# Transposes of activations moved from TensorE to VectorE, in 32 x 32 squares, in a hybrid transformer block

## The chip, the cores and the metric

The kernel runs on one core of a Trainium2 chip. The metric is the device time of one execution in microseconds (us), the median of several runs. The profile is of one execution; its times are in us from the span's start.

## What is computed

One block of a transformer on 256 tokens of width 2048, all in float32. `h = rmsnorm(x)` is multiplied by a wide matrix; a first branch (four heads, a gated linear attention in chunks of 128 tokens) and a second branch (eight heads of differential attention) come out of it, are gated and added; an output projection goes onto the residual stream, and a feed-forward part with a convolution along the tokens follows.

```python
proj = h @ w_in
a_qk, a_v, a_o, a_if, b_q, b_k, b_v, g_a, g_b = split(proj)
h_m = rmsnorm(mlstm_chunkwise(q_m, k_m, v_m, i_pre, f_pre), mlstm_norm_g)
y_a = sigmoid(a_o) * h_m
q_d, k_d = rmsnorm(b_q, q_norm_g), rmsnorm(b_k, k_norm_g)      # per head, 128 features
y_b = diff_attention(q_d, k_d, v_d, lam, lam_init, subln_g)
x = x + (sigmoid(g_a) * y_a + sigmoid(g_b) * y_b) @ w_out
h = rmsnorm(x, norm2_g)
u_g, u_v = split(causal_dwconv(h @ w_up))
x = x + (silu(u_g) * u_v) @ w_down
```

## The kernel before

Every float32 product is made of three products of float32r numbers: an operand is split into a high part (rounded to float32r) and a low part (what is left), and high x high, high x low and low x high are added up in PSUM. The weights are split as they are streamed: `load_chunk` (L80) loads a raw chunk of 1 MB (512 rows by 512 columns, three buffers), and for each of its two halves ScalarE casts the high part `whi` (L90) and VectorE subtracts it from the raw half, which gives the low part `wlo` (L91). There are four buffers of half chunks for each part.

TensorE's queue is in the order in which the program is written (`manual_schedule`); those of the other engines are put in order by a scheduler, with the preparation of weights 100 instructions ahead of other work (`AHEAD`). `t_block` (L101) makes a block of 256 tokens by 512 columns: four chunks, each of two halves of 12 products (L112 to L114). `f_group` (L118) and `wide_group` (L625) do the same with features on the partitions. After each half `slots.tick()` counts one tick and runs the side work that was put down for it with `slots.after(n, ...)`: small products, transposes and what follows them stand between the halves of the main stream.

A mixer (L527, four of them, each for one head of the first branch and two of the second one) has seven blocks: the first branch's values, the second branch's queries, keys and values, and three gates. Where an activation with tokens on the partitions is needed with features there, TensorE transposes it 128 x 128 at a time against an identity, into a PSUM bank `side`:

- `qk_norm` (L447): queries and keys are normed on VectorE to `qn` [128, 2, 4, 128] (L458). Four ticks later `turn` (L461) transposes them, eight times (L465), and ScalarE writes them, scaled by the gain, to `qT` or `kT` (L466).
- the end of `mixer`: the mixed states `hm` of 512 features. Four ticks later `turn` (L565) transposes them, eight times (L570); ScalarE casts the high part `yh` (L574), VectorE subtracts for the low part `yl` (L575). The output projection (L592 on) reads those of mixer j in its chunk j; the last mixer's are made in the projection's first block.
- the residual stream after each of the projection's four blocks: `x2` is added up on VectorE (L601), three ticks later `turn` (L607) transposes 512 features, eight times (L613), and ScalarE and VectorE write both parts, scaled by the norm's gain, for the feed-forward part (L143, L144). Its first group reads the parts of block n in its chunk n.

The load of `x` into `x2` (L598) is issued from ScalarE's queue. The attention weights are transposed on TensorE too (L501); so they are in the changed kernel.

Of the kernel before, what the change touches and what calls it, by code (L numbers as in the profile page):

```python
# [11 lines left out]
F32 = mybir.dt.float32  # L12
F32R = mybir.dt.float32r
AF = mybir.ActivationFunctionType
ALU = mybir.AluOpType
# [10 lines left out]
BH, BD = 8, 128  # L26
# column offsets in w_in
O_AV = 2 * AH * AQK
# [8 lines left out]
BIG = 1e30  # L37
# how far the preparation of weights goes ahead of other work, in instructions
AHEAD = 100


class Slots:
    """Side work placed between the half chunks of the main stream of products."""

# [18 lines left out]
def block_kernel(ctx: ExitStack, tc, x, xT, w_in, ifb, qkw, mg, qg, kg, dl, sg, w_out,  # L63
# [14 lines left out]

# [1 line left out]
    def load_chunk(dmas, ahead=AHEAD):  # L80
# [20 lines left out]
    def t_block(w, col, ah, al):  # L101
        """[tokens, 512] = act.T @ w[:, col:col+512], act as [K, tokens] in parts."""
        ps = [acc(), acc()]
        for c in range(4):
            parts = col_chunk(w, c, col)
            for i in range(2):
                for k in (2 * i, 2 * i + 1):
                    whi, wlo = parts[k]
                    first, last = c == 0 and k == 0, c == 3 and k == 3
                    for t in range(2):  # L110
                        tok = slice(t * P, (t + 1) * P)
                        nc.tensor.matmul(ps[t], ah[c][:, k, tok], whi, start=first, stop=False)  # L112
                        nc.tensor.matmul(ps[t], ah[c][:, k, tok], wlo, start=False, stop=False)  # L113
                        nc.tensor.matmul(ps[t], al[c][:, k, tok], whi, start=False, stop=last)  # L114
                slots.tick()
        return ps

    def f_group(load, ah, al, ps=None, chunks=range(4)):  # L118
        """four tiles [128 features, tokens], two to a bank."""
        ps = ps or [acc(), acc()]  # L120
# [15 lines left out]

# [1 line left out]
    def xtiles(c):  # L138
# [6 lines left out]

# [1 line left out]
    warm = const.tile([P, 1], F32, name="warm")  # L147
# [37 lines left out]

# [1 line left out]
    ident = const.tile([P, P], F32, name="ident")  # L187
# [20 lines left out]
    def rstd(out_, ss, n, count):  # L208
        """(ss / count + EPS) ** -0.5, [P, n]"""
        nc.vector.tensor_scalar(out_, ss, 1.0 / count, EPS, ALU.mult, ALU.add)  # L210
        nc.gpsimd.tensor_tensor(out_, out_, mhalf[:, :n], ALU.pow)

    def row_norm(ssq, name):
        """sums of squares [P, 2, 4] -> rs [P, 2] and its rows on all partitions [P, S]"""
        rs = const.tile([P, 2], F32, name=name)
# [44 lines left out]

    # -lambda
    dlb = start.tile([P, 4, BD], F32, name="dlb")
# [16 lines left out]

    # the masks, and the distances of the keys  # L280
    dist = const.tile([P, S], F32, name="dist")
# [4 lines left out]

# [1 line left out]
    tus = [const.tile([P, 2, 3 + S], F32, name=f"tu{i}") for i in range(3)]  # L288
# [8 lines left out]
    def conv(pool, src, rsb, w, ft, taps):  # L297
        """causal convolution along the tokens of two feature tiles [P, 2, S], scaled by rsb"""
        tu = next_tu()
# [14 lines left out]
    def heads(g, ps):  # L314
        for b in range(2):
# [3 lines left out]
            nc.scalar.activation(o, cv, AF.Silu)  # L319
            qk[2 * g + b] = o          # feature tiles 4g+2b, 4g+2b+1: one head  # L320

    def qk_group(g):
        heads(g, f_group(lambda c: col_chunk(w_in, c, g * 512), hh, hl))

# [1 line left out]
    gate = {}  # L326

    def gates():
        # columns 0..3: i, 32..35: f, as they are; 64..67, 96..99: what their float32r parts leave
        ws = []  # L330
# [8 lines left out]
        def rows():  # L339
# [8 lines left out]
            for n, r in enumerate((li, f)):  # L348
# [3 lines left out]
                nc.vector.tensor_scalar_add(r, r, ib[:, n:n + 1])  # L352
            # log sigmoid: min(f, 0) - log(1 + exp(-|f|))
            nc.scalar.activation(e, f, AF.Abs)
            nc.scalar.activation(e, e, AF.Exp, scale=-1.0)
            nc.scalar.activation(e, e, AF.Ln, bias=1.0)
            nc.vector.scalar_tensor_tensor(lf, f, 0.0, e, ALU.min, ALU.subtract)
            # b: sums of lf in each chunk; a = li - b; mx: running maximum of a, with the carried one
            rows3 = pa.tile([AH, 2 * S + S + P], F32, tag="yb", name="rows3")
# [5 lines left out]
            nc.vector.tensor_tensor(a[:, :S], li, b, ALU.subtract)  # L365
            # the keys of the first chunk as the second one sees them
            nc.vector.tensor_scalar_add(a[:, S:], a[:, :P], b[:, P - 1:P])
# [24 lines left out]

# [1 line left out]
    def mlstm(j, v, hm):  # L394
        """hm [P, 2, 512]: normed states of head j"""
        gb = pa.tile([P, AV], F32, tag="gb", name="gb", bufs=1)
# [3 lines left out]
        kw = dict(skip_group_check=True)  # L400
        # blocks (keys, queries): (0, 0), (1, 1), (0, 1)
        for n, mx in enumerate(gate["mx"]):
# [42 lines left out]

# [1 line left out]
    def qk_norm(ps, gain, dst, wait):  # L447
        """tokens on partitions -> normed, [128, 4, tokens]"""
        st = pa.tile([P, 2, 4], F32, tag="st", name="st", bufs=2)
# [10 lines left out]

        def turn():  # L461
            for t in range(2):
                pt = side()
                for g in range(4):
                    nc.tensor.transpose(pt[:, g * P:(g + 1) * P], qn[:, t, g], ident)  # L465
                nc.scalar.activation(dst[:, :, t * P:(t + 1) * P],  # L466
                                     pt.rearrange("p (g s) -> p g s", s=P), AF.Copy, scale=gain[:, 0:1])
        slots.after(wait, turn)

# [1 line left out]
    scale = BD ** -0.5  # L471
# [51 lines left out]

# [1 line left out]
    yh, yl = [], []  # L525

    def mixer(j):  # L527
# [9 lines left out]
        kT = pa.tile([P, 4, S], F32, tag="kT", name="kT")  # L537
        qk_norm(t_block(w_in, O_BQ + j * 512, hh, hl), qgc, qT, 4)
        qk_norm(t_block(w_in, O_BK + j * 512, hh, hl), kgc, kT, 4)
        ps = t_block(w_in, O_BV + j * 512, hh, hl)  # L540
# [23 lines left out]

        def turn():  # L565
            for n in range(2):
                pt = side()
                for m in range(2):
                    for t in range(2):
                        nc.tensor.transpose(pt[:, m * S + t * P:m * S + (t + 1) * P],  # L570
                                            hm[:, t, (2 * n + m) * P:(2 * n + m + 1) * P], ident)
                o = slice(2 * n, 2 * n + 2)
                pv = pt.rearrange("p (m s) -> p m s", s=S)
                nc.scalar.copy(hi[:, o], pv)  # L574
                nc.vector.tensor_tensor(lo[:, o], pv, hi[:, o].bitcast(F32), ALU.subtract)  # L575
        slots.after(4, turn)

# [9 lines left out]

# [1 line left out]
    p2 = ExitStack()  # L589
    ss2 = const.tile([P, 2, 4], F32, name="ss2")  # L590
    z = []
    for n in range(4):  # L592
# [13 lines left out]

        def turn(n=n, hi=hi, lo=lo):  # L607
            for b in range(2):
                pt = side()
                for m in range(2):  # L610
                    k = 4 * n + 2 * b + m
                    for t in range(2):
                        nc.tensor.transpose(pt[:, m * S + t * P:m * S + (t + 1) * P],  # L613
                                            x2[:, t, k * P:(k + 1) * P], ident)
                for m in range(2):
                    k = 4 * n + 2 * b + m
                    split_scaled(hi[:, 2 * b + m], lo[:, 2 * b + m], pt[:, m * S:(m + 1) * S],
                                 g2c[:, k:k + 1])
        slots.after(3, turn)
    p3.close()  # L620
    rs2, rsb2, spread2 = row_norm(ss2, "rs2")
    slots.after(7, spread2)

# [1 line left out]
    def wide_group(w, col, bank):  # L625
        """four tiles [128 features, tokens], one to a bank, from both parts of z side by side:
        the first half of a bank holds hi * hi + lo * hi, the second one hi * lo"""
        ps = [bank() for _ in range(4)]
# [14 lines left out]
    def ffn_conv(ps, ft):  # L643
        """-> two tiles [P, 2, S]"""
        res = []
# [23 lines left out]
    ps = [[acc() if n < 2 else side() for t in range(2)] for n in range(4)]  # L669
    # two k tiles at once where banks come free, and where they are left, one after the other  # L670
    for ks in [(0, 1)] + [(k,) for k in range(2, NFT - 2)] + [(NFT - 2, NFT - 1)]:
# [63 lines left out]
```

## Time and profile before

| | |
|---|---|
| median of 3 runs | 1604.93 us (1604.55 to 1605.22) |
| span of the profiled execution | 1603.3 us; the page gives no other time of it |
| TensorE (PE) busy | 1592.8 us, 99% |
| VectorE (DVE) busy | 1005.6 us, 63% |
| ScalarE (ACT) busy | 832.1 us, 52% |
| GpSimd (POOL) busy | 35.0 us |
| HBM read | 297.44 MB, 187 GB/s over the span |

Busy time of an engine is the union of its instructions. TensorE's products overlap (a product of 512 columns is shown with 0.39 us, while the next one starts 0.23 us after it), so what a product costs is read from start to start. PEld is TensorE's load of the stationary operand, which runs beside the products. An idle time in brackets names the instruction whose end released it.

### The profile page before, as it was taken

Reading aid. Unit: us, or ns where it says so; the run is one execution under the profiler, and the core shown is the slowest. Engines: PE = TensorE matmul, PEld = TensorE weight load, DVE = VectorE, ACT = ScalarE, POOL = GpSimd, SP = SyncE. Lnnn points to the kernel's source line nnn. Section 1 sums busy time; section 2 is a strip of 40 time slices with the busy share of each in tenths; the row PEclk is TensorE's granted clock in tenths of the full one; section 3 lists DMA queues with packets and bytes.
Section 4 is the critical chain, followed back from the end, with each engine's and each line's share of the span. In section 5 each row is a group of like instructions: output and inputs, shape, how many; then the busy total and the mean of one; then the engine's idle time right before and its main releaser. Section 6 shows DMA issues by size and latency. Waiting matters only on the chain.

```text
span 1603.3 us, 20531 instructions
## 1 busy us (share of the span) xinstructions
PE 1592.8 (99%) x8149; PEld 1353.8 (84%) x8149; DVE 1005.6 (63%) x1372; ACT 832.1 (52%) x1135; POOL 35.0 (2%) x54
## 2 busy tenths in 40 slices
PE   8999999999999999999999999999999999999998
PEld 8988888888988888888888888888888888888887
DVE  6865655565655655566555776677767776655554
ACT  6754545454554555455444655555555555444442
POOL 0000000000000000100000000000000000000000
PEclk9999999999999999999999999999999999999999
DMA  9655455545555455554655555555555555555553
GB/s 306 210 192 190 162 195 175 184 166 188 174 181 190 164 187 177 182 184 166 240 176 181 185 186 188 188 189 190 187 184 184 184 184 186 199 193 186 204 187 132
DMA packets 138553, 300.88 MB, mean 188 GB/s; under 512 B 9816, under 2 KB 12120, under 8 KB 132312
## 3 DMA queue, kind: packets, MB, share of 16 engines
q1 hardware_dynamic: 137720, 296.41, 54.7%
q10 hardware_dynamic: 416, 2.11, 0.4%
q0 software_dynamic: 320, 1.05, 0.3%
q8 instruction: 64, 1.05, 0.3%
q14 instruction: 33, 0.27, 0.0%
HBM read 297.44 MB, written 2.10 MB: 187 GB/s over the span
## 4 chain that ended last, share of the span: by engine, by line
PE 98%; DMA 1%; SPq 0%; DVE 0%; ACT 0%; issue 0%
PE acc L112 15%; PE acc L114 15%; PE acc L113 15%; PE side L636 10%; PE acc L636 10%; PE side L638 5%; PE acc L638 5%; PE acc L687 2%; PE acc L688 2%; PE side L688 2%; PE side L687 2%; PE acc L689 2%; PE side L689 2%; PE acc L133 2%; PE acc L131 2%; PE acc L132 2%
## 5 line engine op out<-in xcount | busy, mean ns | idle before, releaser
L91 DVE TENSOR_TENSOR wlo<-raw,whi 128x1024 fp32r<-128x1024 f32 x548 | 670.0, 1224 | 483.3 <-ACT whi L90 481.0
L90 ACT CAST whi<-raw 128x1024 fp32r<-128x1024 f32 x548 | 575.4, 1051 | 634.3 <-PE acc L114 289.0
L112 PE MATMUL acc<-whi,x 128*128 128x512 f32 x896 | 352.8, 394 | 0.0
L114 PE MATMUL acc<-whi,x 128*128 128x512 f32 x896 | 349.4, 390 | 0.0
L113 PE MATMUL acc<-wlo,x 128*128 128x512 f32 x896 | 349.1, 390 | 0.0
L636 PE MATMUL side<-x,whi 128*128 128x512 f32 x704 | 249.2, 399 | 0.0
L636 PE MATMUL acc<-x,whi 128*128 128x512 f32 x704 | 249.2, 399 | 0.0
L114 PEld LDWEIGHTS acc<-whi,x 128*128 128x128 f32 x896 | 168.2, 188 | 35.5
L638 PE MATMUL side<-x,wlo 128*128 128x256 f32 x704 | 197.7, 281 | 0.0
L638 PE MATMUL acc<-x,wlo 128*128 128x256 f32 x704 | 197.5, 281 | 0.0
L112 PEld LDWEIGHTS acc<-whi,x 128*128 128x128 f32 x896 | 168.3, 188 | 34.1
L113 PEld LDWEIGHTS acc<-wlo,x 128*128 128x128 f32 x896 | 168.4, 188 | 33.5
L636 PEld LDWEIGHTS side<-x,whi 128*128 128x128 f32 x704 | 132.3, 188 | 33.0
L636 PEld LDWEIGHTS acc<-x,whi 128*128 128x128 f32 x704 | 132.3, 188 | 32.8
L638 PEld LDWEIGHTS side<-x,wlo 128*128 128x128 f32 x704 | 133.0, 189 | 0.0
L638 PEld LDWEIGHTS acc<-x,wlo 128*128 128x128 f32 x704 | 132.9, 189 | 0.0
L308 DVE SCALAR_TENSOR_TENSOR cv<-tu,fwc,cv 128x256 f32<-128x256 f32 x176 | 73.4, 479 | 0.0
L687 PE MATMUL acc<-whi,ah 128*128 128x512 f32 x176 | 68.5, 389 | 0.0
L689 PE MATMUL acc<-whi,al 128*128 128x512 f32 x176 | 68.5, 389 | 0.0
L688 PE MATMUL acc<-wlo,ah 128*128 128x512 f32 x176 | 68.5, 389 | 0.0
L687 PE MATMUL side<-whi,ah 128*128 128x512 f32 x176 | 68.5, 389 | 0.0
L688 PE MATMUL side<-wlo,ah 128*128 128x512 f32 x176 | 68.5, 389 | 0.0
(209 smaller groups left out, 1646.4 us busy)
## 6 DMA issues: line engine op xcount, KB each, us to landing
raw<-w_in SPq DMA_DIRECT2D x126, 1024.0 KB, 4.9
raw<-w_up SPq DMA_DIRECT2D x88, 1024.0 KB, 5.0
raw<-w_down SPq DMA_DIRECT2D x44, 1024.0 KB, 4.8
raw<-w_out SPq DMA_DIRECT2D x16, 1024.0 KB, 5.0
wr<-w_in SPq DMA_DIRECT2D x8, 256.0 KB, 4.2
xs<-x SPq DMA_DIRECT2D x2, 1024.0 KB, 9.6
x<-x ACTq DMA_DIRECT2D x1, 2048.0 KB, 8.3
out<-x SPq DMA_DIRECT2D x8, 256.0 KB, 2.4
```

The costliest lines, as they stand in the source:

```text
L90: nc.scalar.copy(hi, r)
L91: nc.vector.tensor_tensor(lo, r, hi.bitcast(F32), ALU.subtract)
L112: nc.tensor.matmul(ps[t], ah[c][:, k, tok], whi, start=first, stop=False)
L113: nc.tensor.matmul(ps[t], ah[c][:, k, tok], wlo, start=False, stop=False)
L114: nc.tensor.matmul(ps[t], al[c][:, k, tok], whi, start=False, stop=last)
L131: nc.tensor.matmul(o, whi, ah[c][:, k, :], start=st, stop=False, **kw)
L308: nc.vector.scalar_tensor_tensor(cv[:, f], tu[:, f, 3 - d:3 - d + S], wf[:, j:j + 1], cv[:, f], ALU.mult, ALU.add)
L636: nc.tensor.matmul(ps[f], whi, z[c][:, k].rearrange("p t s -> p (t s)"), start=first, stop=last, skip_group_check=True)
L638: nc.tensor.matmul(ps[f][:, :S], wlo, z[c][:, k, 0], start=False, stop=last, skip_group_check=True)
L687: nc.tensor.matmul(ps[n][t], h_, whi, start=k == 0, stop=False)
L688: nc.tensor.matmul(ps[n][t], h_, wlo, start=False, stop=False)
L689: nc.tensor.matmul(ps[n][t], l_, whi, start=False, stop=k == NFT - 1)
```

## The change

A helper `block_turn` transposes 256 tokens by 512 features on VectorE: a transpose of VectorE turns squares of 32 x 32 within 32 partitions, so 16 instructions, one for each pair of a group of 32 partitions of the source and one of the destination, each of eight squares, put the squares where they belong. Queries and keys, mixed states and residual use it right where they are made, not in a slot some ticks later; ScalarE scales queries and keys in place (one instruction of 1024 elements a partition instead of two of 512 from PSUM), and the parts of the mixed states and of the residual are made from the transposed tile in SBUF. The tile of the mixed states, `yt`, takes the buffer of `kT`; `zt` is new, with two buffers. Comments are left out of the file as well, so its line numbers are other ones.

```diff
+    def block_turn(dst, src):
+        v = dst.rearrange("p m (t s) -> p t m s", t=2)
+        for a in range(4):
+            for b in range(4):
+                nc.vector.transpose(v[32 * b:32 * b + 32, :, :, 32 * a:32 * a + 32],
+                                    src[32 * a:32 * a + 32, :, :, 32 * b:32 * b + 32])
...
-    def qk_norm(ps, gain, dst, wait):
+    def qk_norm(ps, gain, dst):
...
-        def turn():
-            for t in range(2):
-                pt = side()
-                for g in range(4):
-                    nc.tensor.transpose(pt[:, g * P:(g + 1) * P], qn[:, t, g], ident)
-                nc.scalar.activation(dst[:, :, t * P:(t + 1) * P],
-                                     pt.rearrange("p (g s) -> p g s", s=P), AF.Copy, scale=gain[:, 0:1])
-        slots.after(wait, turn)
+        block_turn(dst, qn)
+        nc.scalar.activation(dst, dst, AF.Copy, scale=gain[:, 0:1])
...
-        def turn():
-            for n in range(2):
-                pt = side()
-                for m in range(2):
-                    for t in range(2):
-                        nc.tensor.transpose(pt[:, m * S + t * P:m * S + (t + 1) * P],
-                                            hm[:, t, (2 * n + m) * P:(2 * n + m + 1) * P], ident)
...
-                nc.scalar.copy(hi[:, o], pv)
-                nc.vector.tensor_tensor(lo[:, o], pv, hi[:, o].bitcast(F32), ALU.subtract)
-        slots.after(4, turn)
+        yt = pa.tile([P, 4, S], F32, tag="kT", name="yt")
+        block_turn(yt, hm.rearrange("p t (m f) -> p t m f", f=P))
+        nc.scalar.copy(hi, yt)
+        nc.vector.tensor_tensor(lo, yt, hi.bitcast(F32), ALU.subtract)
...
-        def turn(n=n, hi=hi, lo=lo):
-            for b in range(2):
-                pt = side()
...
-                        nc.tensor.transpose(pt[:, m * S + t * P:m * S + (t + 1) * P],
-                                            x2[:, t, k * P:(k + 1) * P], ident)
...
-        slots.after(3, turn)
+        zt = pb.tile([P, 4, S], F32, tag="zt", name="zt", bufs=2)
+        block_turn(zt, x2[:, :, cs].rearrange("p t (m f) -> p t m f", f=P))
+        for m in range(4):
+            split_scaled(hi[:, m], lo[:, m], zt[:, m], g2c[:, 4 * n + m:4 * n + m + 1])
```

How the instructions stand on the engines is shown at three places. The first is VectorE after the block of queries in the first mixer; before, low parts alone stand behind the second `qn`:

```order
L458 TENSOR_TENSOR qn<-acc,st 128x512
L91 TENSOR_TENSOR wlo<-raw,whi 128x1024
L458 TENSOR_TENSOR qn<-acc,st 128x512
L91 TENSOR_TENSOR wlo<-raw,whi 128x1024 x6
L453 TENSOR_REDUCE st<-sq 128x4
```

and with the change (L398 is the transpose in `block_turn`, L466 the norming):

```order
L466 TENSOR_TENSOR qn<-acc,st 128x512
L398 STREAM_TRANSPOSE qT<-qn 32x2x4x32 x2
L91 TENSOR_TENSOR wlo<-raw,whi 128x1024
L398 STREAM_TRANSPOSE qT<-qn 32x2x4x32 x5
L91 TENSOR_TENSOR wlo<-raw,whi 128x1024
L398 STREAM_TRANSPOSE qT<-qn 32x2x4x32 x5
L91 TENSOR_TENSOR wlo<-raw,whi 128x1024
L398 STREAM_TRANSPOSE qT<-qn 32x2x4x32 x4
L91 TENSOR_TENSOR wlo<-raw,whi 128x1024 x3
L461 TENSOR_REDUCE st<-sq 128x4
```

Sixteen transposes stand among the same six low parts, three of which come between them.

The second place is ScalarE at the same point, with the change. L460 is the square of the norm, L470 the scaling by the gain:

```order
L460 ACTIVATE sq<-acc,rs_577 128x512
L90 CAST whi<-raw 128x1024 x5
L470 ACTIVATE qT<-qT,qgc 128x1024
L90 CAST whi<-raw 128x1024 x2
L460 ACTIVATE sq<-acc,rs_577 128x512
```

Before, two scalings (L466) stood behind four casts and waited for TensorE; now one stands behind five casts and waits for VectorE.

The third place is VectorE from the end of the last mixer through the output projection's first block, with the change (L561 adds the branches, L570 is the low part `yl`, L595 adds the residual `x_6619`, which is `x2`):

```order
L561 TENSOR_TENSOR hm<-hm,yb 128x512
L91 TENSOR_TENSOR wlo<-raw,whi 128x1024
L398 STREAM_TRANSPOSE yt<-hm 32x2x4x32 x5
L91 TENSOR_TENSOR wlo<-raw,whi 128x1024
L398 STREAM_TRANSPOSE yt<-hm 32x2x4x32 x5
L91 TENSOR_TENSOR wlo<-raw,whi 128x1024
L398 STREAM_TRANSPOSE yt<-hm 32x2x4x32 x5
L91 TENSOR_TENSOR wlo<-raw,whi 128x1024
L398 STREAM_TRANSPOSE yt<-hm 32x2x4x32
L91 TENSOR_TENSOR wlo<-raw,whi 128x1024
L570 TENSOR_TENSOR yl_6456<-yt,yh_6455 128x1024
L91 TENSOR_TENSOR wlo<-raw,whi 128x1024 x4
```

Before, four low parts stood between the last addition and the two instructions for `yl`. On ScalarE the cast of `yh` now stands behind five casts of weights, and the load of `x` behind one more cast and with a wait for VectorE.

## Rows read from the trace of the kernel before

**Rows 1.** The page: busy time by engine, granted clock in slices, the chain's shares.
```profile
span 1603.3 us, 20531 instructions
...
PE 1592.8 (99%) x8149; PEld 1353.8 (84%) x8149; DVE 1005.6 (63%) x1372; ACT 832.1 (52%) x1135; POOL 35.0 (2%) x54
...
PEclk9999999999999999999999999999999999999999
...
PE 98%; DMA 1%; SPq 0%; DVE 0%; ACT 0%; issue 0%
```
**Rows 2.** The table of waits: us in total, times, longest.
```profile
DVE wlo L91 <- ACT whi L90: 481.0, 388, 3.2
ACT whi L90 <- PE acc L114: 289.0, 200, 2.4
```
**Rows 3.** Groups by line on PE: count | busy us, mean ns | idle before.
```profile
L465 PE MATMUL side<-ident,qn 128*128 128x128 f32 x64 | 8.3, 272 | 0.0
...
L613 PE MATMUL side<-ident,x 128*128 128x128 f32 x32 | 4.1, 272 | 0.0
L570 PE MATMUL side<-ident,hm 128*128 128x128 f32 x32 | 4.1, 272 | 0.0
```
**Rows 4.** Instructions in order of time, first mixer: start, us, engine, line.
```profile
118.06 0.39 PE L113 MATMUL acc<-wlo,x 128*128 128x512 f32 x1
118.28 0.39 PE L114 MATMUL acc<-whi,x 128*128 128x512 f32 x1
...
119.62 0.40 PE L113 MATMUL acc<-wlo,x 128*128 128x512 f32 x1
```
**Rows 5.** The same in the output projection's first block.
```profile
778.29 0.39 PE L114 MATMUL acc<-whi,yl 128*128 128x512 f32 x1
...
779.63 0.40 PE L113 MATMUL acc<-wlo,yh 128*128 128x512 f32 x1
```
**Rows 6.** Groups by line on DVE.
```profile
L91 DVE TENSOR_TENSOR wlo<-raw,whi 128x1024 fp32r<-128x1024 f32 x548 | 670.0, 1224 | 483.3 <-ACT whi L90 481.0
...
L651 DVE TENSOR_TENSOR u<-acc,u 128x256 f32<-128x256 f32 x44 | 17.0, 423 | 0.4 <-ACT u L650 0.4
...
L144 DVE SCALAR_TENSOR_TENSOR x<-side,g2c,x 128x256 fp32r<-128x256 f32 x16 | 7.0, 478 | 0.6 <-ACT x L143 0.6
...
L601 DVE TENSOR_TENSOR x<-acc,x 128x512 f32<-128x512 f32 x8 | 5.2, 682 | 0.0
```
**Rows 7.** DVE in order of time, feed-forward part.
```profile
906.23 1.12 DVE L651 TENSOR_TENSOR u<-side,u 128x256 f32<-128x256 f32 x3
```
**Rows 8.** DVE and ACT in order of time, queries of the first mixer.
```profile
114.76 0.68 DVE L458 TENSOR_TENSOR qn<-acc,st 128x512 f32<-128x512 f32 x1
...
118.71 1.05 ACT L90 CAST whi<-raw 128x1024 fp32r<-128x1024 f32 x1 [1.67 <-PE acc L114]
...
119.79 1.23 DVE L91 TENSOR_TENSOR wlo<-raw,whi 128x1024 fp32r<-128x1024 f32 x1 [1.49 <-ACT whi L90]
```
**Rows 9.** DVE and ACT in order of time, last mixer's end; the load's landing.
```profile
771.41 1.22 DVE L91 TENSOR_TENSOR wlo<-raw,whi 128x1024 fp32r<-128x1024 f32 x1
...
778.72 1.05 ACT L90 CAST whi<-raw 128x1024 fp32r<-128x1024 f32 x1 [1.75 <-PE acc L114]
779.60 0.39 ACTq L598 DMA_DIRECT2D x<-x  x1
...
DMA to landing us min/median/max: 8.3/8.3/8.3
```
**Rows 10.** PE and ACT in order of time, first feed-forward group.
```profile
860.43 0.39 PE L636 MATMUL acc<-x,whi 128*128 128x512 f32 x1
...
868.83 1.04 PE L613 MATMUL side<-ident,x 128*128 128x128 f32 x8
...
869.86 0.83 ACT L143 ACTIVATE x<-side,g2c 128x256 fp32r<-128x256 f32 x2
```
**Rows 11.** DMA issues: count, KB each, median us to landing.
```profile
raw<-w_in SPq DMA_DIRECT2D x126, 1024.0 KB, 4.9
```

More of the change, by code (lines that the diff above doesn't have):

```diff
@@ L537, in mixer @@
         kT = pa.tile([P, 4, S], F32, tag="kT", name="kT")
-        qk_norm(t_block(w_in, O_BQ + j * 512, hh, hl), qgc, qT, 4)
-        qk_norm(t_block(w_in, O_BK + j * 512, hh, hl), kgc, kT, 4)
+        qk_norm(t_block(w_in, O_BQ + j * 512, hh, hl), qgc, qT)
+        qk_norm(t_block(w_in, O_BK + j * 512, hh, hl), kgc, kT)
         ps = t_block(w_in, O_BV + j * 512, hh, hl)
@@ L563, in mixer @@
         yl.append(lo)
-        def turn():
-            for n in range(2):
-                pt = side()
-                for m in range(2):
-                    for t in range(2):
-                        nc.tensor.transpose(pt[:, m * S + t * P:m * S + (t + 1) * P],
-                                            hm[:, t, (2 * n + m) * P:(2 * n + m + 1) * P], ident)
-                o = slice(2 * n, 2 * n + 2)
-                pv = pt.rearrange("p (m s) -> p m s", s=S)
-                nc.scalar.copy(hi[:, o], pv)
-                nc.vector.tensor_tensor(lo[:, o], pv, hi[:, o].bitcast(F32), ALU.subtract)
-        slots.after(4, turn)
+        yt = pa.tile([P, 4, S], F32, tag="kT", name="yt")
+        block_turn(yt, hm.rearrange("p t (m f) -> p t m f", f=P))
+        nc.scalar.copy(hi, yt)
+        nc.vector.tensor_tensor(lo, yt, hi.bitcast(F32), ALU.subtract)
     gates()
@@ L605, in block_kernel @@
         z.append(both)
-        def turn(n=n, hi=hi, lo=lo):
-            for b in range(2):
-                pt = side()
-                for m in range(2):
-                    k = 4 * n + 2 * b + m
-                    for t in range(2):
-                        nc.tensor.transpose(pt[:, m * S + t * P:m * S + (t + 1) * P],
-                                            x2[:, t, k * P:(k + 1) * P], ident)
[L615 to L618, printed above, removed]
-        slots.after(3, turn)
+        zt = pb.tile([P, 4, S], F32, tag="zt", name="zt", bufs=2)
+        block_turn(zt, x2[:, :, cs].rearrange("p t (m f) -> p t m f", f=P))
+        for m in range(4):
+            split_scaled(hi[:, m], lo[:, m], zt[:, m], g2c[:, 4 * n + m:4 * n + m + 1])
     p3.close()
```

## The prediction

> **What bounds the kernel now.** I read the page first: TensorE is busy in 1592.8 of 1603.3 us, its clock is granted at full speed (the 2.4 GHz level) in every slice, and the chain that ended last is TensorE for 98% [rows 1]. So an instruction that leaves TensorE's stream shortens the kernel by what it takes there, as long as nothing else comes to hold TensorE up. What could is seen in the table of waits: VectorE waits for ScalarE's high parts and ScalarE waits for TensorE to give a weight buffer back [rows 2]. The weights are thus prepared as early as the four buffers allow, and VectorE, busy for 63%, has idle time behind every low part [rows 1, 2]. There is no transfer to reckon with as a bound: the chain has 1% of DMA [rows 1].
>
> **What leaves TensorE.** 64 + 32 + 32 = 128 transposes [rows 3], in 16 groups of 8. What a group takes is read from starts around it: from the last product before it (118.28) to the second after it (119.62) are 1.34 us [rows 4], where two undisturbed steps would take 2 x 0.226 (118.06 to 118.28 is one of them), so 0.89 us. The first group of the output projection lies in the same way between 778.29 and 779.63 with steps of 0.233: 0.87 us [rows 5]. 16 x 0.88 = **14.1 us** come off. All of it counts, as TensorE's queue is written by hand and the products behind a group move up.
>
> **What VectorE gets.** 16 bursts (four for queries, four for keys, four for the mixed states, four for the residual) of 16 instructions, 256 in all, each over 32 partitions and 256 elements in each of them. No row of before shows this operation. Rows of 256 elements bound it: 0.423 us for an addition, 0.478 for a scaled subtraction [rows 6]; three independent additions in a run start 0.35 apart (1.12 us for three, the last taking 0.42) [rows 7]. If a transpose went at half pace it would cost like a row of 512 elements, 0.682, at a quarter like one of 1024, 1.224 [rows 6]. I take **0.42**, the row with the same number of elements and one element at a time, for a transpose moves each element once, and none overlapped with the next; ends of the range are 0.35 and 1.22. 256 x 0.42 = 107.5 us more on VectorE, whose share goes from 63% to about 69%.
> The Trainium skill, VectorE: DVE Perf Modes, section "Two Vector instructions with no wait between them", says that an instruction starts only when all earlier ones are done if its output or input begins in another group of 32 partitions than the last one's; each of these does. By it the 0.35 of overlapping additions doesn't apply and 0.42 does; with 0.35 the sum below would be 0.5 us lower.
> The same page, section "The three transpose paths", gives VectorE 311 ns for 128 columns of 16-bit data; 128 columns more would make it an estimate of 0.44 us, and the sum 0.4 us higher.
>
> **What hides it.** A half chunk of weights is cast as soon as the half four before it has been used up: ScalarE 1.05, VectorE 1.23 [rows 8]; TensorE needs it after three more halves of 12 products, 3 x 2.72 = 8.15 us. So a low part may come 8.15 - 1.05 - 1.23 = 5.8 us late. VectorE's queue is in order, and the new order puts one low part between at most five transposes in most bursts (5 x 0.42 + 1.23 = 3.3 us a tick of 2.72), so each burst falls behind and catches up after it.
> Queries, first mixer: the second qn ends at 115.44 [rows 8]. 16 transposes and the three low parts between them take 6.7 + 3.7: 125.8. On ScalarE the scaling by the gain stands behind five casts and before the next, which is due at 118.71 + 2 x 2.72 = 124.15 [rows 8]. It runs 125.8 to 126.9 (1.05, as the cast of 1024 elements), the cast to 127.9, the low part to 129.2; TensorE needs that half at 124.15 + 8.15 = 132.3. **3.1 us are left**, so nothing is lost. The keys come out alike; their products with the queries come only after the next block of eight ticks, 21.8 us.
> Mixed states of mixers 0 to 2: nobody on TensorE reads them before the output projection, and the cast behind them stays on time. Nothing. The last mixer's are read in the very next block, by its last chunk. There the low part after the last addition ends at about 772.6, and then the casts come 2.8 us apart (12 products of 0.233; 778.72 is one [rows 9]): five transposes to 774.7, low part, five to 778.0, low part, five to 781.3, low part to 782.55, one to 783.0; ScalarE casts yh to 784.05, VectorE subtracts yl (after one more low part) to 785.4. TensorE's chunk 3 starts after 72 products of 0.233 from 767.3 (the 48th starts at 778.29 [rows 5]): 784.1, and the wait for yl sits at its second product, 784.35. **1.1 us of stall**, where before there was none.
> Residual: the load of x now stands in ScalarE's queue behind that yl, so it goes at 785.4 instead of 779.6 [rows 9], lands 8.3 later (793.7), and VectorE asks for it only after a low part that ends at about 796. Nothing. The first three bursts run like that of the queries. The first addition ends at 796.8, a low part at 798.9, the second addition at 799.6; 16 transposes and two low parts end at 808.8, four scaled copies by ScalarE (two take 0.83 [rows 10]) at 810.5. The cast due at 778.72 + 10 x 2.8 + 1.1 = 807.8 waits for them and gives its low part at 812.9; needed at 816.2, 3.3 left. The fourth is read by chunk 3 of the first feed-forward group, which starts at 860.43 + 6 x 2.8 = 877.2 (868.83 - 860.43 are three ticks [rows 10]); the last addition ends at 861.4, 16 transposes and three low parts at 871.8, and the four low parts of z at 874.9. 2.3 left. DMA issues move with the low parts that free the raw buffers, by no more than the 3 to 4 us above; a raw chunk lands in 4.9 us [rows 11] and is wanted some 11 after its buffer is freed (five halves of 2.72, less the low part's 2.3). ScalarE's and VectorE's own splits stay in number of elements; their cost is nothing where they are hidden as before.
>
> **Sum.** 1603.3 - 14.1 + 1.1 = 1590.3 us of span. The median of the runs is 1604.93, 1.6 above the span of the profiled execution, and nothing in the change touches what lies around it: **1591.9 us**, 0.8% faster. With x = 16 x (T - 0.42) the stall is 1.1 + x, and from x = 2.3, 3.1 and 3.3 on also the last residual burst, the eight of queries and keys and the three first of the residual lose what is over: T = 0.48 gives 1592.9, T = 0.60 1595.4, T = 0.64 1600.
>
> **Rivals.** (1) A transpose goes at half pace, 0.69: x = 4.3, and the bursts lose 8 x 1.2 + 3 x 1.0 + 2.0 + 5.4 = 20.2 us, **1611 us**, slower; at a quarter pace, 1.22, it would be about 1742 (x = 12.8: 8 x 9.7 + 3 x 9.5 + 10.5 + 13.9, and three mixed bursts at about 7). It decides from T = 0.66 on, where the loss is the 14.1 us gained. For it: the operation has no row, and 8 transposes that cost TensorE 0.88 us cost VectorE 6.7. Against it: all rows that move one element at a time agree on one price. The Trainium skill, VectorE: DVE Perf Modes, section "Rules for kernel authors", would leave a 128 x 128 transpose to TensorE where PSUM will do as its place; its preference speaks for this rival, and the rows agree on the engines' time (0.11 us against 0.84 for one), not on who has it to spare.
> (2) The replay is too kind: in-order queues on two engines, and each burst gives back the 0.9 us that it saves by some low part that comes late. Then **1605**, no change. For it: margins of 2 to 3 us on 10 us of burst; against it: the waits that VectorE and ScalarE show now are each other's and TensorE's, 481 and 289 us of them [rows 2], so there is time to catch up in.
> (3) No stall at all, if yl is earlier than I have it: 1591, inside the forecast's range.
> That the transposes stay on TensorE cannot be: its order lists none of the three lines any more.
>
> **How the numbers follow.** Forecast (with 3) 0.83, rival 1 0.12, rival 2 0.05. The range goes from 1590 (no stall, and 1 us for a gain read a little short) to 1600 (T = 0.64); with rival 1 and the upper half of 2 outside it holds a little over 8 in 10. About 0.2% (3.2 us) is what a measurement of this kernel can tell from no change. Faster 0.83, same 0.05, slower 0.12.
>
> **What would show it.** In the changed profile: 8149 - 128 products on TensorE; transposes at 0.35 to 0.48 us; one gap of TensorE near 774 (784 less eleven groups), of 1 to 2 us, released by VectorE's yl; none in the mixers. Wrong if TensorE shows gaps at low parts behind the bursts, 8 times the same, or if its granted clock falls.

## The result, and the profile after

| | before | changed |
|---|---|---|
| executions, us | six, 1604.55 to 1607.44 | 1583.51, 1583.54, 1583.70, 1592.00, 1592.56, 1592.60 |
| median | 1605.08 | 1587.85 |
| profiled execution / its span | / 1603.3 | 1592.0 / 1590.2 |
| predicted | | 1591.9 (1590 to 1600) / 1590.3 |

The kernel is faster by about 1%, ratio 0.9899 (95%: 0.9879 to 0.9918). But no execution took the median: the changed kernel has two levels, 1592.4 and 1583.6, 8.8 us apart. The upper one is within 0.5 us of the forecast; the median of both lies 2.1 us below the range. Compared like with like, as worked out below, the change is worth 12.5 to 12.7 us, 0.8%. The profiled execution is at the upper level, so it can be compared with the sum term by term. Line numbers below are those of the changed kernel.

The page of the changed kernel, against [rows 1]:
```profile
span 1590.2 us, 20513 instructions
...
PE 1579.3 (99%) x8021; PEld 1340.8 (84%) x8021; DVE 1112.8 (70%) x1624; ACT 827.8 (52%) x1123; POOL 35.8 (2%) x54
...
PEclk9999999999999999999999999999999999999999
...
PE 97%; DVE 1%; DMA 1%; SPq 0%; ACT 0%; issue 0%
```
8149 - 128 = 8021 products; VectorE is busy for 107 us more; the clock is granted in full in every slice, and the chain is TensorE's still. The groups by line on DVE (count | busy us, mean ns | idle before) price the transpose that no row of before had:
```profile
L91 DVE TENSOR_TENSOR wlo<-raw,whi 128x1024 fp32r<-128x1024 f32 x548 | 668.4, 1223 | 363.5 <-ACT whi L90 359.9
...
L398 DVE STREAM_TRANSPOSE qT<-qn 32x256 f32<-32x256 f32 x64 | 27.9, 436 | 1.2
```
It takes 436 ns, and so do the 64 of the keys, the mixed states and the residual: 256 x 0.436 = 111.7 us. The waits (total, times, longest) show what they displaced:
```profile
DVE wlo L91 <- ACT whi L90: 359.9, 303, 4.0
...
ACT whi L90 <- PE acc L114: 234.5, 164, 3.1
...
ACT qT L470 <- DVE qT L398: 16.0, 4, 4.0
...
ACT x L143 <- DVE zt L398: 14.0, 4, 4.9
```
VectorE's wait for high parts fell from 481.0 [rows 2] to 359.9: the transposes fill idle time. ScalarE now waits behind each burst for up to 4.9 us. That reaches TensorE once only. DVE in order of time, queries of the first mixer (start, us):
```profile
114.36 0.68 DVE L466 TENSOR_TENSOR qn<-acc,st 128x512 f32<-128x512 f32 x1
115.08 0.88 DVE L398 STREAM_TRANSPOSE qT<-qn 32x256 f32<-32x256 f32 x2
115.99 1.23 DVE L91 TENSOR_TENSOR wlo<-raw,whi 128x1024 fp32r<-128x1024 f32 x1
117.25 2.23 DVE L398 STREAM_TRANSPOSE qT<-qn 32x256 f32<-32x256 f32 x5
119.52 1.23 DVE L91 TENSOR_TENSOR wlo<-raw,whi 128x1024 fp32r<-128x1024 f32 x1
...
124.29 1.79 DVE L398 STREAM_TRANSPOSE qT<-qn 32x256 f32<-32x256 f32 x4
```
Two, five, five and four transposes with a low part between: the burst ends at 126.08, predicted 125.8. Counted from the end of the second qn (115.04 here, 115.44 before) it takes 11.0 us where 10.4 were predicted. Five take 2.23, about 0.45 from start to start at 0.436 each: none overlaps the next, as the Trainium skill, VectorE: DVE Perf Modes, section "Two Vector instructions with no wait between them", says. TensorE works through this stretch (us, then busy time and count of PE, PEld, DVE, ACT, POOL; granted clock):
```profile
104.00:152.00 48.00, 48.00 (x214) 39.74 (x213) 39.43 (x64) 22.52 (x24) 3.36 (x3) 1.00 0.55 181
```
VectorE does 39.43 of 48 us, and TensorE is busy for 48.00. The one stall, PE in order of time at the output projection:
```profile
773.74 0.39 PE L114 MATMUL acc<-whi,yl 128*128 128x512 f32 x1
774.53 0.50 PE L112 MATMUL acc<-whi,yh 128*128 128x512 f32 x1 [0.41 <-ACT yh L569]
774.87 0.40 PE L113 MATMUL acc<-wlo,yh 128*128 128x512 f32 x1
775.85 0.50 PE L114 MATMUL acc<-whi,yl 128*128 128x512 f32 x1 [0.58 <-DVE yl L570]
776.18 0.40 PE L112 MATMUL acc<-whi,yh 128*128 128x512 f32 x1
```
TensorE is idle for 0.41 us before yh and 0.58 before yl, 1.0 in all. What the stall costs is more, by the starts: the four steps from 773.74 to 776.18 take 2.44 us, where four of 0.233 would take 0.93, so **1.5 us** are lost, where 1.1 were predicted; the step behind each wait is 0.33, 0.10 longer than the others. Behind its first 20 us TensorE has no other gap. In these 20 us, ahead of all that was changed, it waits once for a low part in both traces, 0.76 us before and 0.30 with the change.

### The profile page after: what moved, and what is told of

Read it like the earlier page. It is cut to its first block, busy times and chain, and to the rows that moved or that the text cites. A ratio compares the mean times of both kernels' runs of the same rounds, so it can differ in the third digit from the quotient of the medians.

```text
span 1590.2 us, 20513 instructions
## 1 busy us (share of the span) xinstructions
PE 1579.3 (99%) x8021; PEld 1340.8 (84%) x8021; DVE 1112.8 (70%) x1624; ACT 827.8 (52%) x1123; POOL 35.8 (2%) x54
## 4 chain that ended last, share of the span: by engine, by line
PE 97%; DVE 1%; DMA 1%; SPq 0%; ACT 0%; issue 0%
PE acc L114 14%; PE acc L112 14%; PE acc L113 14%; PE side L621 10%; PE acc L621 10%; PE acc L623 5%; PE side L623 5%; PE side L674 3%; PE acc L674 3%; PE acc L673 3%; PE side L673 3%; PE acc L672 3%; PE side L672 3%; PE acc L133 2%; PE acc L132 2%; PE acc L131 2%
## 5 line engine op out<-in xcount | busy, mean ns | idle before, releaser
L91 DVE TENSOR_TENSOR wlo<-raw,whi 128x1024 fp32r<-128x1024 f32 x548 | 668.4, 1223 | 363.5 <-ACT whi L90 359.9
L113 PE MATMUL acc<-wlo,x 128*128 128x512 f32 x896 | 349.0, 390 | 0.0
L113 PEld LDWEIGHTS acc<-wlo,x 128*128 128x128 f32 x896 | 168.3, 188 | 33.9
```

Of the source, the lines that this page charges most:

```text
L91: nc.vector.tensor_tensor(lo, r, hi.bitcast(F32), ALU.subtract)
```

## Where the two levels lie

I split the spans by the first product of each stage. The second trace is of the same kernel at the lower level (run again2, below):

| us | mixers | output projection | feed-forward | down projection |
|---|---|---|---|---|
| before | 767.3 | 93.1 | 498.5 | 244.3 |
| changed, upper level | 757.2 | 91.1 | 497.6 | 244.3 |
| changed, lower level | 757.2 | 91.1 | 489.0 | 244.3 |

The change shows as 10.1 + 2.0 + 0.9 = 13.0 us, of which 0.46 are the shorter wait near 20 us, which is not of its making. The levels differ in the feed-forward part alone; the changed kernel has no transposes on TensorE there, the kernel before one group of eight. There wide_group gives TensorE a product of 512 columns and one of 256 in turn. PE in order of time, upper level:
```profile
1099.64 0.40 PE L621 MATMUL side<-x,whi 128*128 128x512 f32 x1
1099.88 0.28 PE L623 MATMUL side<-x,wlo 128*128 128x256 f32 x1
1099.99 0.40 PE L621 MATMUL side<-x,whi 128*128 128x512 f32 x1
...
1101.40 0.40 PE L621 MATMUL side<-x,whi 128*128 128x512 f32 x1
```
and at the lower level:
```profile
1099.82 0.40 PE L621 MATMUL side<-x,whi 128*128 128x512 f32 x1
1100.05 0.28 PE L623 MATMUL side<-x,wlo 128*128 128x256 f32 x1
1100.17 0.39 PE L621 MATMUL side<-x,whi 128*128 128x512 f32 x1
...
1101.56 0.39 PE L621 MATMUL side<-x,whi 128*128 128x512 f32 x1
```
The busy times are alike; the starts are not. Five pairs take 1.76 us above (1099.64 to 1101.40) and 1.74 here; over a group of 64 pairs it is 353.33 ns a pair against 346.67. That holds for all but the first 56 of the 1408 pairs: 1352 x 6.66 ns = 9.0 us. The first 56, in the first group, go the other way, with 346.7 in the trace of the upper level and 353.3 in that of the lower, which takes back 0.4: 8.6, as by the stages. The rhythm changes at four small products in the first group (L225, which spread the norm's factors). PE in order of time there, upper level:
```profile
865.69 0.39 PE L621 MATMUL acc<-x,whi 128*128 128x512 f32 x1
...
867.42 0.39 PE L621 MATMUL acc<-x,whi 128*128 128x512 f32 x1
...
867.77 0.61 PE L225 MATMUL side<-diag,ones 128*128 128x128 f32 x4
...
868.57 0.39 PE L621 MATMUL acc<-x,whi 128*128 128x512 f32 x1
...
870.33 0.40 PE L621 MATMUL acc<-x,whi 128*128 128x512 f32 x1
```
Five pairs take 1.73 us ahead of the four products and 1.76 behind them. No wait and no clock is behind the levels. Windows of the upper level, columns as above:
```profile
860.00:1350.00 490.00, 490.00 (x2772) 424.99 (x2771) 353.76 (x509) 270.36 (x376) 1.60 (x1) 1.00 0.57 187
```
and of the lower:
```profile
860.00:1350.00 490.00, 490.00 (x2812) 428.13 (x2811) 358.39 (x520) 275.42 (x383) 1.60 (x1) 1.00 0.58 191
```
Both have TensorE busy throughout at a granted clock of 1.00 (2.4 GHz); the lower one gets 40 products more into the same 490 us.

## The experiments

**The changed kernel again**, unedited, in two later sessions.

> The changed kernel once more, for its two levels: six executions gave 1583.5 to 1583.7 and 1592.0 to 1592.6 us. Theory A (the working of the prediction holds for one level, 1591.9, and a second effect worth 8.7 us shows in some executions): levels at 1583.6 and 1592.3 again, nothing between. Theory B (the low level belonged to the first chip or session): one level alone, 1592.3 or 1583.6. If the profiled execution falls on the low level, its trace differs from the first one by 8.7 us in one stage or in the step of the products.

Measured: 1591.64 to 1593.54 in all six, median 1592.74, ratio 0.9933 (0.9909 to 0.9957). Of the 24 executions of before beside it two took 1596.08 and 1595.84, the rest about 1605. So before has the lower level too.

> The changed kernel in a third session, to see whether its share of the low level differs from that of the kernel before beside it. Theory R: both kernels show the same two levels, 8.9 us apart (1592.3 and 1583.5; 1605.0 and 1596.0), and like is to be compared with like: 12.6 us between the high levels and between the low ones. Rival: the change itself makes the low level its rule, then most executions at 1583.5 while those of before stay at 1605.0.

Measured: 1583.35, 1583.78, 1583.90, 1592.39, 1592.59, 1592.78; the profile is at the lower level, span 1581.6, and is the second trace above. Of the 17 of before four took 1595.97 to 1596.89. Over all sessions I saw the lower level in 14 of 67 executions of before and 6 of 18 of the changed kernel: too few to say that the change makes it likelier.

**One part of the change alone**, three kernels, each with the old code for the other two parts:
```
QK_DVE, HM_DVE, X_DVE = True, False, False    # only_qk; only_hm and only_x likewise
if not QK_DVE:
    ...
    nc.tensor.transpose(pt[:, g * P:(g + 1) * P], qn[:, t, g], ident)
    ...
```


> Queries and keys alone on VectorE: eight groups of transposes off TensorE, 8 x 0.88 = 7.1 us, nothing lost behind the bursts: 1598.0 us. If the second level of the changed kernel comes from this part, some executions lie 8.7 lower, at 1589.3; if the bursts cost something by themselves, above 1599.

> Mixed states alone: four groups off, 3.5 us, and 1.0 us of wait for the last mixer's low part: 1602.5 us, with one gap of TensorE near 782. If the second level comes from this part, some executions at 1593.8.

> Residual alone: four groups off, no wait: 1605.0 - 3.5 = 1601.5 us. If the second level comes from this part, some executions at 1592.8.

Measured: only_qk 1597.55 to 1598.64 in nine of ten (one at 1589.47), median 1598.22; only_hm 1603.0 to 1605.6 in seven of ten (three at 1594.3 to 1594.6), median 1603.27; only_x 1592.4 to 1592.98 in all five, its profile at the lower level. Like with like, against 1605.0 and 1596.0: -6.8 for queries and keys, about -1.6 for the mixed states, -3.3 for the residual, 11.7 together. Laid product against product (the traces have the same 8021 products in the same order, the transposes aside), the removed groups give back 0.87 to 0.90 us each: 7.2, 3.5 - 1.5 for the stall, and 3.5, so 12.7 together. The medians lie 0.2 to 0.4 below that in each part. In the traces of only_qk and only_hm 0.3 to 0.4 of it lies in the first 20 us, ahead of the change, and in that of only_hm another 0.3 near 798. The stall comes with them alone, PE in order of time of only_hm:
```profile
782.43 0.50 PE L113 MATMUL acc<-whi,yh 128*128 128x512 f32 x1 [0.40 <-ACT yh L594]
...
783.74 0.50 PE L115 MATMUL acc<-whi,yl 128*128 128x512 f32 x1 [0.58 <-DVE yl L595]
```
0.40 and 0.58, as with the whole change. only_x would have read as 12 us of gain, had its level not been looked at. It also shows that the odds of the level may depend on the program: all five executions of only_x were at the lower one, and of the kernel before, beside it, two of 24.

**The levels taken away.** In wide_group the four products of 512 columns of a k go first, then the four of 256, in the changed kernel and in before alike:
```
 for f in range(4):
-    whi, wlo = (t[:, f * P:(f + 1) * P] for t in parts[k])
+    whi = parts[k][0][:, f * P:(f + 1) * P]
     nc.tensor.matmul(ps[f], whi, ...)
+for f in range(4):
+    wlo = parts[k][1][:, f * P:(f + 1) * P]
     nc.tensor.matmul(ps[f][:, :S], wlo, ...)
```


> The changed kernel, and in the feed-forward groups the four products of 512 columns first, then the four of 256, in place of one and one. Theory R (the two levels are two rhythms into which TensorE's alternating products of the feed-forward part fall, 353.3 or 347.0 ns a pair, for 1408 pairs): with the alternation gone there is one level; a pair costs 227 + 113 to 120, 340 to 347 ns, so 1592.3 - 8.9 = 1583.4 us at most and 1574 at best, without a spread of 9 us. Rival D (the levels come from the memory or another engine, in whatever order the products stand): two levels 8.9 us apart stay.

> The same order of products in the kernel before. Theory R: one level too, and as far under 1605.0 as the run with the changed kernel is under 1592.3; the two runs then differ by what the change itself is worth, 14.1 - 1.1 = 13.0 us, without the rhythm. If the change is worth more than that apart from the rhythm, the difference is larger.

Measured: pairs4 1588.83 to 1590.45 in six, median 1589.50, ratio 0.9914 (0.9892 to 0.9936); pairs4_before 1601.87 to 1602.56 in ten, median 1602.05, ratio 0.9999 (0.998 to 1.0018; 8 of the 20 executions of before beside it were at 1595.45 to 1596.64). Each kernel now has one level, between the two: the alternation is what makes them. I had expected the lower level or less, which was wrong. What the pair of kernels gives is the change by itself: 1602.05 - 1589.50 = **12.55 us**.

With two and two (pairs2):

> The changed kernel with two products of 512 columns and then their two of 256. If what costs in the feed-forward part is each change from one width to the other (half as many here, a quarter with four and four, which had 351.1 ns a pair), a pair costs about 350, one level near 1588. If the rhythm is what counts, it is a level of its own between 347.0 and 353.3, that is 1583.5 to 1592.5, in all executions.

Measured: 1585.36 to 1586.22 in four, median 1585.62, ratio 0.9891 (0.986 to 0.9921), one level again. PE in order of time:
```profile
1099.69 0.63 PE L622 MATMUL side<-x,whi 128*128 128x512 f32 x2
1100.16 0.39 PE L626 MATMUL side<-x,wlo 128*128 128x256 f32 x2
1100.38 0.62 PE L622 MATMUL side<-x,whi 128*128 128x512 f32 x2
```
0.69 us for two pairs here, 349 ns each from its stage of 491.1 us; pairs4 has 351. So the price is not one for each change of width: a quarter as many changes cost more than half as many. This version is below both kernels' medians, though not below the changed kernel's lower level, and has none of their spread of 9 us.

**What picks the level.** An unused product of 128 columns ahead of each of the 22 groups interrupts the alternation:
```
+nc.tensor.matmul(ps[0][:, :P], ones, ident, start=True, stop=True, skip_group_check=True)
 for c in range(4):
```


> The changed kernel with one small product (128 x 128, not used) ahead of each of the 22 feed-forward groups. Theory R with the rhythm set anew by every interruption: rhythms of both kinds within one execution, group by group; times between 1583.5 and 1592.5 plus 22 x 0.2 to 0.4 us, so 1588 to 1601, and not two levels 8.9 us apart. Rival: one rhythm in all 22 groups of an execution, then something outside TensorE's stream sets it.

Measured: 1588.14, 1588.79, 1588.95, 1589.59, 1591.04, 1596.56, 1598.74. In the profiled one (span 1587.0) the first group steps at 353.3 ns a pair up to the four products of L225, and all that follows at 346.7. So the small product doesn't draw the rhythm anew for each group, and it doesn't bring one level either. The four products do change it: in all eight traces that reach them without a wait in the feed-forward part (before, after, again, again2, the three parts and reset) the first group has one rhythm up to them and the rest the other one, from 346.7 to 353.3 five times at the upper level and from 353.3 to 346.7 three times. The eight transposes that stand in the first group of before, only_qk and only_hm don't change it. So an execution's level goes with the rhythm in which its first group starts; what decides that is open, and another slot for the four products was not tried.

**How much cover there is.** Each transpose done twice:
```
+for _ in range(2):
     nc.vector.transpose(v[32 * b:32 * b + 32, :, :, 32 * a:32 * a + 32],
```


> The changed kernel with each of the 256 transposes done twice: 112 us more on VectorE, whose share goes from 70% to about 77%. Theory A (a burst has 2.3 to 3.3 us of cover left, and what is over is lost): 7.0 us more a burst, so 4 to 5 us lost in each of the eight of queries and keys, about 4 in each of the four of the residual, 8 at the last mixer, some 60 us in all: 1640 to 1660. Rival B (an engine busy for 77% has room): no more than 7 us, those of the last mixer, 1599.

Measured, in one execution: 1711.74, with a span of 1710.0, 119.8 us more. The page:
```profile
PE 1613.4 (94%) x8021; PEld 1362.2 (80%) x8021; DVE 1223.3 (72%) x1880; ACT 830.0 (49%) x1123; POOL 35.8 (2%) x54
```
DVE in order of time at the queries of the first mixer:
```profile
125.21 9.19 DVE L399 STREAM_TRANSPOSE qT<-qn 32x256 f32<-32x256 f32 x20
134.43 4.63 DVE L91 TENSOR_TENSOR wlo<-raw,whi 128x1024 fp32r<-128x1024 f32 x4
```
PE by line, what it waited for:
```profile
L113 PE MATMUL acc<-wlo,x 128*128 128x512 f32 x896 | 358.2, 400 | 51.8 <-DVE wlo L91 51.8
```
PE in order of time around that gap:
```profile
129.91 0.39 PE L112 MATMUL acc<-whi,x 128*128 128x512 f32 x1
135.71 0.79 PE L113 MATMUL acc<-wlo,x 128*128 128x512 f32 x1 [5.41 <-DVE wlo L91]
136.30 0.63 PE L114 MATMUL acc<-whi,x 128*128 128x512 f32 x1
...
139.71 0.52 PE L113 MATMUL acc<-wlo,x 128*128 128x512 f32 x1
140.07 0.40 PE L114 MATMUL acc<-whi,x 128*128 128x512 f32 x1
```
and windows behind it:
```profile
136.00:140.00 4.00, 4.00 (x10) 3.13 (x10) 3.66 (x4) 1.09 (x2) 0.00 (x0) 0.50 0.52 157
140.00:145.00 5.00, 5.00 (x23) 4.11 (x23) 1.99 (x3) 2.69 (x3) 1.31 (x1) 1.00 0.78 294
```
VectorE's share is only 72%, yet TensorE stands still 18 times more than in the kernel before, 86.1 us in all: for low parts (14 times, 69.3), for yh and yl (9.1) and in the first feed-forward group (7.6). The direction was right, the size was not: I had reckoned with the changed kernel's order, five transposes between low parts, and the scheduler put 20 in a row, 9.19 us. The other 34 us came with the gaps: after 5.41 us of idling TensorE's granted clock is 0.50 (the 1.2 GHz level), and 1.00 again from about 140. Nine steps take 4.00 us (135.71 to 139.71) where 9 x 0.227 = 2.04 would do, so some 2 us go behind this gap. There are 14 stretches at 0.50 in this trace, and TensorE is busy for 63.3 us of them; at half the clock, half of that is lost, an estimate of 31.6 us, nearly all of the 34.

**Where cover is missing.** From pairs4, the transposes of the attention weights go to VectorE as well, where TensorE's next products wait for them:
```
+for a_ in range(4):
+    for b_ in range(4):
+        nc.vector.transpose(pd[32 * b_:32 * b_ + 32, :, 32 * a_:32 * a_ + 32],
+                            sd[32 * a_:32 * a_ + 32, :, 32 * b_:32 * b_ + 32])
...
-    nc.tensor.transpose(pt[:, n * P:(n + 1) * P], pw[:, 0, n * P:(n + 1) * P], ident)
```


> On top of four and four (1589.5 us, one level): the 24 transposes of the attention weights, the last ones of activations on TensorE, go to VectorE too, 16 bursts of 16 instructions of 32 or 64 elements, some 0.2 us each, so 3 to 4 us a burst. On TensorE the 16 groups cost 119 and 228 ns, 2.8 us in all. Theory A (a burst is hidden as long as its low parts keep within the 5.8 us): 1586.7 us. Rival B (the attention blocks have VectorE and ScalarE already waiting for each other, and each burst loses over 0.2 us): 1590 to 1610.

Measured: 1603.88 to 1609.28 in twelve, median 1607.93, 18.4 us above pairs4 and ratio 1.0027 (1.001 to 1.0043) to before: the whole gain is gone. Its waits:
```profile
ACT ath L509 <- DVE pw L504: 56.0, 16, 4.8
```
PE by line:
```profile
L113 PE MATMUL acc<-wlo,x 128*128 128x512 f32 x896 | 351.8, 393 | 5.5 <-DVE wlo L91 5.5
...
L517 PE MATMUL side<-bvh,ath 128*128 128x256 f32 x24 | 8.4, 348 | 5.4 <-ACT ath L509 5.4
...
L519 PE MATMUL side<-bvh,atl 128*128 128x256 f32 x24 | 7.5, 311 | 2.6 <-DVE atl L510 2.6
```
and windows:
```profile
200.00:215.00 15.00, 12.99 (x52) 10.26 (x51) 10.44 (x20) 8.15 (x11) 1.42 (x2) 0.89 0.44 143
```
24 transposes left TensorE, at 0.117 us some 2.8. In return it stands idle for 13.5 us at 16 places, four in each mixer: at products that read the transposed weights (L517, L519) and at low parts that come late behind the burst (L113). Laid product against product, three of the mixers lose 5.2 us each and one 3.6. The three have a stretch of 3.4 us at a granted clock of 0.50 behind the gaps (the 0.89 above is the mean over 15 us with one), the fourth has none; TensorE is busy in it, so by estimate 1.7 us go there. That is the difference between the mixers, and the executions show it too: they lie at about 1604.0, 1605.8, 1607.5 and 1608.7, with mean granted clocks of 1.000, 0.999, 0.998 and 0.997.

## Why the prediction was wrong, point by point

**What was right** is the mechanism, and the terms hold nearly one by one. "16 x 0.88 = 14.1 us come off": 14.2, product against product (7.2, 3.5 and 3.5). "I take 0.42": 0.436, so that x = 0.26 us by its formula. The Trainium skill, VectorE: DVE Perf Modes, section "The three transpose paths", had given 0.44 as an estimate, with the 128 columns more: the trace's 0.436 agrees. "1.1 us of stall", 1.4 by its formula at 0.436: 1.5 measured by the starts, 1.0 of it idle, at 774.5 and 775.9, where "near 774" was said, released by yh as well as by yl. "3.1 us are left" and the other margins: no other gap behind the bursts. Thus the change by itself should give 14.2 - 1.5 = 12.7 us; it gave 12.55 between the two kernels with one level each, 12.5 between the upper levels and 12.6 between the lower ones. That the profiled execution came to 1592.0, where 1591.9 was forecast, is in part luck: its wait near 20 us was 0.46 shorter than in the trace of before. The twelve executions at the upper level, of all three sessions, have a median of 1592.6.

**What failed** is the step "The median of the runs is 1604.93, 1.6 above the span of the profiled execution, and nothing in the change touches what lies around it", with the range's lower end, "no stall, and 1 us for a gain read a little short". It took the rest of TensorE's stream for something that has one duration. It has two, 8.6 us apart in the feed-forward part: the three executions of before that I had were all at the upper one, the changed kernel drew three of each, and the median fell between. That it fell there was a matter of the draw: in the run again all six were at the upper level, inside the range. The executions of before beside again, again2 and pairs4 show that the lower level isn't the change's work, for 14 of 67 have it without the change. The trace of before had a sign of it that I did not follow: its first feed-forward group steps at about 347 ns a pair, up to the four products of the norm, and the later ones at 353.3, the same products at two rates under a clock of 1.00. The stall, 0.4 us larger than its term, is the only other miss of size, and doesn't matter for the range. (By the prediction's own formula T = 0.64 gives 1600.7, not 1600; nothing hangs on that.)

**The rivals.** Half pace (0.69) fell to 0.436. That the replay is too kind fell to TensorE's 48.00 of 48.00 us around a burst. No stall fell to 1.5. But twice and attn_dve show how near the first two are: with bursts of double length the same move costs 119.8 us, so what decides is the 3 us left behind each burst and not the 30% that VectorE is idle. The rule that a 128 x 128 transpose belongs to TensorE (the Trainium skill, VectorE: DVE Perf Modes, section "Rules for kernel authors") is right by the engines' time, 0.11 us against 16 x 0.436 / 8 = 0.87, and it is right for the attention weights, where 2.8 us off TensorE cost 18.4 in all. For the four uses of this change the measurement goes against it, since VectorE's 111.7 us were idle time and TensorE's 14.2 were not.

## What to carry to other kernels

Work on the bounding engine costs its time from start to start around it, and moving it to an engine eight times slower for it pays where the next reader is far and each burst fits the slack of one buffer round; reckon that slack per burst, in the order that the scheduler really issues, not from busy shares. A burst that overruns costs more than its length, for behind the 5.41 us gap TensorE ran on at half the granted clock for 4 us. Before one compares two kernels by medians, look whether either has levels: split the traces by stage and compare the stage that the change doesn't touch.

## What was not expected of the hardware

TensorE ran one unbroken stream of 512- and 256-column products in two rhythms, 353.3 or 346.7 ns a pair, at a granted clock of 1.00 in both, and kept to one for over 450 us; two of each in turn gave about 349, four of each 351, always the same. In eight traces of eight the rhythm changed once, at the same four products of 128 columns in the first group. What picks the rhythm with which an execution starts stays open.
